# Attention weights of the last token tile transposed by VectorE and a round trip through DRAM, in a two-layer decoder trunk on one Trainium2 core

## The chip, the cores and the metric

The kernel runs on one core of a Trainium2 chip. The metric is the device time of one execution in microseconds (us), lower is better. Engines are named as in the profile: PE is TensorE (PEld its weight loads), DVE is VectorE, ACT is ScalarE, POOL is GpSimd, SP is SyncE, which here only issues DMAs.

## The reference

A trunk of two layers, each followed by a squared-ReLU MLP. Layer 0 mixes tokens by causal pooling, layer 1 by stick-breaking attention, with 16 heads of 64 and keys and values projected once from the stream behind layer 0. SEQ is 512, D_MODEL 1024, D_FF 4096, all in float32.

```python
def stick_breaking_attention(q, k, v):
    for i in range(S // Q_BLOCK):
        ...
        z = jnp.einsum('bhqd,bhkd->bhqk', q_blk, k_blk, ...) * inv_sqrt_d
        mask = s_idx < t_idx
        log1m = jnp.where(mask, -jax.nn.softplus(z), 0.0)
        excl = lax.cumsum(log1m, axis=3, reverse=True) - log1m
        a = jnp.where(mask, jnp.exp(jax.nn.log_sigmoid(z) + excl), 0.0)
        outs.append(jnp.einsum('bhqk,bhkd->bhqd', a, v_blk.astype(jnp.float32)))

def reference(x, ...):
    for layer in range(DEPTH):
        h = rms_norm(x, mix_pre_g[layer])
        m = ...                      # pooling (layer 0), or attention and w_o (layer 1)
        x = x + rms_norm(m, mix_post_g[layer])
        h = rms_norm(x, mlp_pre_g[layer])
        x = x + rms_norm(sq_relu_mlp(h, w_up[layer], w_down[layer]), mlp_post_g[layer])
        if layer == N_A - 1:
            kv = jnp.matmul(rms_norm(x, kv_norm_g), w_kv)...
    return x
```

## The kernel before

The 512 tokens are T = 4 tiles of 128. A float32 operand is split in two parts, hi (a cast, on ACT, L414) and lo (the rest, a subtraction on DVE, L415), and a product of two such operands is three products on PE (hi hi, hi lo, lo hi). The MLPs and the projections take most of the span.

The attention works on 8 pairs of heads. Its order is written out by hand in the table ATT_ORDER: each entry is a letter, a pair and sometimes a head of the pair (0 or 1), and a loop issues the entries one after the other under a manual schedule of all five engines. So the table alone sets the order on each engine. The letters that matter:

- S: scores of a pair (L1202), 24 products on PE into six PSUM banks, in three groups (token tile 3; tile 2; tiles 1 and 0); three rounds for each tile (hi hi, q hi with k lo, q lo with k hi), the two heads in turn
- G: sigmoids of the scores on ACT, `u` (L1216) and `w` (L1220) for both heads
- X: the running product along the keys, a scan on DVE over 1280 columns (L1225), into `e`. The 1280 columns are the causal part of a head's 512 x 512 weights, in segments: token tile 3 with 512 keys first, then tile 2 (384), tile 1 (256), tile 0 (128)
- M: `w = w * e` on DVE (L1316): a head's attention weights, tokens on partitions, keys along the columns
- T: the weights are transposed in blocks of 128 x 128 on PE (L1241), ten a head, through three PSUM banks, each copied by ACT (L1243) to a tile `at`: keys on partitions, tokens along the columns
- A: `mix_pair` (L1251), the product of a pair's weights with v: for each of the four key tiles s and each head one matmul over the tokens s*128 to 511, all in one PSUM bank. In float32 a matmul leaves two records in the trace. a: its split into `ohl` (ACT hi, DVE lo)
- J and Q: projections of k and q for a later pair (L842 to L844), 24 products each; j and q: their splits
- L, g, W, w: a weight of a later projection is loaded (SP, L223, into `raw`, `spare` or `late`), scaled by a gain (DVE, L230, 128 x 1024; only those for k and q), cast to hi (ACT, L249) and its lo taken (DVE, L258)
- Z, z: the output projection, 18 products a half and token tile for three pairs of heads

A pair's pieces are spread over two blocks of the table. S, G, X, M of pair p stand in one block with J, Q of pair p+1 and A of pair p-1; T of p closes the block; A of p comes at the end of the next. So on PE the steady order is A(p-1), T(p), S(p+1), J, Q, A(p), and so on. PSUM has eight banks of 128 x 512, given out in turn.

The functions that the change touches:

Of the kernel before, what the change touches and what calls it, by code (L numbers as in the profile page):

```python
# [10 lines left out]
F32 = mybir.dt.float32  # L11
# [4 lines left out]
P = 128  # L16
D = 1024
S = 512
T = S // P
KC = D // P  # L20
# [8 lines left out]
PAIRS = HEADS // 2  # L29
WINDOWS = (2, 4, 8, 16)  # L30
EPS = 1e-6
TS = [slice(t * P, (t + 1) * P) for t in range(T)]
NS = [slice(0, 512), slice(512, 1024)]
# [22 lines left out]
    (w[0], int(w[1:2] or 0), int(w[2:] or 0))  # L56
    for w in """V5 N2 v5 V0 N3 V3 F3 v0 J0 v3 F2 j0 Q0 L L q0 V1 v1 F1 L L V2 v2
    S0 G0 X00 M00 J1 W X01 w V4 M01 j1 T00 T01 W F4 v4 w Q1 q1 V6 v6
    S1 G1 g g X10 M10 X11 J2 L L M11 W j2 w Q2 q2 A0 a0 T10 T11 W
    S2 G2 g g w X20 M20 X21 J3 M21 W j3 w L L Q3 q3 A1 a1 T20 T21 W  # L60
    S3 G3 g g w X30 M30 X31 J4 M31 W j4 w L L Q4 q4 A2 a2 T30 T31 W
    S4 G4 g g w X40 M40 X41 J5 M41 W j5 w L Q5 q5 A3 a3 T40 T41 W
    S5 G5 w L L X50 M50 X51 J6 M51 W j6 w L Q6 q6 A4 a4 T50 T51 W
    S6 G6 w X60 M60 X61 J7 M61 W j7 w L L L Q7 q7 A5 a5 T60 T61 W
    S7 A6 G7 w L X70 Z002 M70 W X71 w Z102 M71 W T70 w R a6 W w L W Z034 Z134 w T71 L W w L Z055 Z155
    W w L A7 W w Z066 Z166 z206 a7 W w s""".split()
]

# [22 lines left out]
def trunk(ctx, tc, x, consts, gcol, grow, pw, wup, wdn, wq, wk, wv, wo, out):  # L91
    nc = tc.nc
# [5 lines left out]
    dram = pool("dram", space=bass.MemoryType.DRAM)  # L98
# [3 lines left out]
    def name(s):  # L102
        uid[0] += 1
        return f"{s}{uid[0]}"

    def ps():
        return psum.tile([P, 512], F32, tag="ps", name=name("ps"))
# [13 lines left out]
    turn = [0]  # L121
# [15 lines left out]
    behind, latest = {}, {}  # L137
# [19 lines left out]
    def gains(lo, n):  # L157


        def scaled(raw):  # L160
            for k in range(n):
                c = raw[:, k * D // n : (k + 1) * D // n]
                nc.scalar.mul(c, c, gc[:, lo + k : lo + k + 1])

        return scaled
# [44 lines left out]
    def late_next(what, fits=lambda x: True):  # L210
        while not fits(late[upto[what]]):
            upto[what] += 1
        upto[what] += 1
        return late[upto[what] - 1]
# [8 lines left out]
        nc.sync.dma_start(raw, x["src"])  # L223
        x["raw"] = raw

    def late_scale():
        x = late_next("g", lambda x: x["wide"] is not None)
        c = x["raw"].rearrange("p (k c) -> p k c", k=KC)
        g = gc[:, x["wide"] : x["wide"] + KC].unsqueeze(2).broadcast_to((P, KC, D // KC))
        nc.vector.tensor_tensor(out=c, in0=c, in1=g, op=ALU.mult)  # L230
# [134 lines left out]
    def fill(n=1):  # L365
        if gate[0]:
            behind.update(latest)
        for _ in range(n):
            if queue and sum(map(in_ring, made)) < ahead and (queue[0][0][0] != "dn" or dn_pool[0]):
                if not any(x["key"] == queue[0][0] for x in late) or queue[0][0] in kept:  # L370
                    make()
# [6 lines left out]
    for l in range(2):  # L378
        if l == 1:
            n = len(queue)  # L380
            for what, i, part in ATT_ORDER:
                if what == "V":
                    for h in range(2):
                        at = VALUES[i][2]
# [82 lines left out]
    class Update:  # L467
# [33 lines left out]
        def product(self, n):  # L501
            return self.beside if n and self.cuts is not NS else self.scaled
# [344 lines left out]
    with tc.tile_pool(name="mix0", bufs=1, reuse_waits="tile") as mp:  # L847
# [163 lines left out]
        def transposed(t, h):  # L1011
            pt = pts[t, h] = ps()
            for c in range(4):
                k = 4 * h + c
                nc.tensor.transpose(pt[:, TS[c]], xns[t][:, k * P : (k + 1) * P], ident)
# [47 lines left out]
    with tc.tile_pool(name="att", bufs=1, reuse_waits="tile") as ap:  # L1063
# [164 lines left out]
            )  # L1228
            return e

        def transposed(w):
            parts = {}
            for tiles in ((0,), (1, 3), (2,)):
                pt = ps()
                c = 0
                turned = ap.tile([P, S], F32, tag="at", bufs=6, name=name("at"))
                for s in tiles:
                    parts[s] = turned, c
                    for i in range(s, T):
                        at = SEG[i][0] + s * P  # L1240
                        nc.tensor.transpose(pt[:, c : c + P], w[:, at : at + P], ident)  # L1241
                        c += P
                latest["act"] = nc.scalar.copy(turned[:, :c], pt[:, :c])  # L1243
            return parts

        def mix_pair(p):
            po = pos[p] = ps()
            for s in range(T):
                for a in range(2):
                    turned, c = parts[p, a][s]  # L1250
                    nc.tensor.matmul(  # L1251
                        po[half[a], s * P :], v_all[:, s, 2 * p + a], turned[:, c : c + S - s * P],
                        start=s == 0, stop=s == T - 1, skip_group_check=True,
                    )

        def mixed_out(p):
            if p < PAIRS - 1:
# [24 lines left out]
        with tc.manual_schedule(engines={on.PE, on.Activation, on.DVE, on.Pool, on.SP}):  # L1282
            for what, i, a in ATT_ORDER:
                if what == "V":
                    value_product(i)
                elif what == "v":
                    value_out(i)
                elif what == "F":
                    form(i)
                elif what == "W":  # L1290
                    late_high()
                    if upto["W"] < 16:
                        fill()
                elif what in "Lgws":
                    {"L": late_load, "g": late_scale, "w": late_low, "s": late_store}[what]()
                elif what == "R":
                    gpost1, gpre1 = gain_row(R_MIX_POST1), gain_row(R_MLP_PRE1, spare_tile())
                elif what == "N":
                    need(i)
                elif what in "JQ":  # L1300
                    project(("k" if what == "J" else "q", i))
                    fill()
                elif what == "j":
                    keys(i)
                elif what == "q":
                    queries(i)
                elif what == "S":
                    pzs[i] = scores((qs[i], ks[i]))
                elif what == "G":
                    for a in range(2):  # L1310
                        ws[i, a] = sigmoids(pzs[i], a)
                elif what == "X":
                    es[i, a] = scanned(a)
                elif what == "M":
                    w = ws[i, a]
                    latest["dve"] = nc.vector.tensor_tensor(out=w, in0=w, in1=es.pop((i, a)), op=ALU.mult)  # L1316
                elif what == "T":
                    parts[i, a] = transposed(ws.pop((i, a)))
                elif what == "A":
                    mix_pair(i)  # L1320
                elif what == "a":
                    mixed_out(i)
                elif what in "Zz":
                    out_product(i, range(a // 10, a % 10 + 1), range(2) if what == "Z" else [0])
            assert upto["W"] == upto["w"] == len(late) and not going, upto
            ups = [Update(t, gpost1, None, gpre=gpre1) for t in range(T)]

            def evacuate(t, n):
                up, bank = ups[t], sums.pop((t, n))
                up.halves = (up.halves or []) + [ap.tile([P, 512], F32, tag="at", bufs=6, name=name("at"))]  # L1330
                up.just_square(n, bank)
                latest["dve"] = nc.vector.tensor_tensor(
                    out=up.halves[n], in0=bank, in1=gpost1[:, NS[n]], op=ALU.mult
                )

            for t in range(2):
                for n in range(2):
                    out_product(t, [PAIRS - 1], [n])
                    evacuate(t, n)
                ups[t].factor()  # L1340
            ups[0].sums_added()
            ups[0].rstd()
            ups[1].sums_added()
            ups[0].norm()
            ups[1].rstd()
            ups[1].norm()
            out_product(2, [PAIRS - 1], [0])
            evacuate(2, 0)
            out_product(2, range(PAIRS), [1])
            evacuate(2, 1)  # L1350
            ups[2].factor()
            out_product(3, range(PAIRS - 2), [0])
            ups[0].transpose()
            ups[2].sums_added()
            out_product(3, range(PAIRS - 2, PAIRS), [0])
            out_product(3, [0], [1])
            ups[1].transpose()
            evacuate(3, 0)
            ups[2].rstd()
            ups[2].norm()  # L1360
            out_product(3, range(1, PAIRS), [1])
            fill(4)
            evacuate(3, 1)
            ups[3].factor()
            ups[3].sums_added()
            ups[3].rstd()
            ups[3].norm()
            pending.update({t: ups[t] for t in (T - 2, T - 1)})
# [68 lines left out]
```

## Time and profile before

| | |
|---|---|
| median of 3 runs (lowest to highest) | 896.77 us (896.38 to 897.31) |
| profiled execution, its own time | 896.91 us |
| its span, first to last instruction | 895.1 us |
| busy: PE, DVE, ACT, POOL | 885.7, 689.4, 520.6, 85.1 us |
| the attention's pairs | one every 17.26 to 17.27 us, from A to A |
| transposes by PE in the attention (L1241) | 160, 19.3 us busy |

The profile's page gives busy times by engine, the chain of work that ended last, groups of instructions by line, and DMA issues with the time until they landed. A timeline row has the start, the duration, engine and line, the output and the inputs, the shape and the number of instructions, and in brackets how long the engine was idle before it and what released it. Times are counted from the span's start.

### The profile page before, as it was taken

The page shows a single profiled execution, that of the slowest core. Times are in us where ns is not written, and L with a number is a line of the kernel's source. Part 1 is how long each engine was busy: PE and PEld are TensorE (multiplying, and loading weights), DVE is VectorE, ACT ScalarE, POOL GpSimd, SP SyncE. Part 2 cuts the span into 40 slices and gives each one's busy share as a digit, 9 for nine tenths or more (in the row PEclk, how much of TensorE's full clock was granted, in tenths as well). Part 3 has the DMA queues.
Part 4 walks back from the last instruction along what each step waited for, and adds up shares of the span by engine and source line. Part 5 has one row for each costly group of instructions (what it writes and reads, how often), then busy time and mean ns, then how long its engine had stood idle before and what let it go on. Part 6 is the DMA issues. An engine that isn't in the chain of part 4 may idle for free.

```text
span 895.1 us, 11808 instructions
## 1 busy us (share of the span) xinstructions
PE 885.7 (99%) x4586; PEld 769.4 (86%) x4586; DVE 689.4 (77%) x705; ACT 520.6 (58%) x842; POOL 85.1 (10%) x83
## 2 busy tenths in 40 slices
PE   9999999999999999999999999999999999999996
PEld 7998888888888888888788888998888888888885
DVE  5966897998979967667887784765797776967866
ACT  6758557566888737345577564475445444544531
POOL 2100000000000005000000000120220400303103
PEclk9999999999999999999999999999999999999999
DMA  7453557369796820976122115333415043142102
GB/s 282 160 206 128 192 191 266 117 227 344 275 340 233 313 78 25 366 267 232 51 71 71 48 69 214 118 119 143 140 57 191 35 147 121 51 164 83 56 15 94
DMA packets 42349, 141.00 MB, mean 158 GB/s; under 512 B 4096, under 2 KB 4570, under 8 KB 42294
## 3 DMA queue, kind: packets, MB, share of 16 engines
q1 hardware_dynamic: 42146, 140.24, 43.7%
q8 instruction: 36, 0.59, 0.3%
q14 instruction: 19, 0.16, 0.1%
q10 hardware_dynamic: 148, 0.02, 0.0%
HBM read 116.12 MB, written 24.12 MB: 157 GB/s over the span
## 4 chain that ended last, share of the span: by engine, by line
PE 97%; DMA 1%; issue 1%; DVE 0%; ACT 0%; POOL 0%; POOLq 0%; DVEq 0%; SPq 0%; ACTq 0%
PE ps L726 28%; PE ps L842 16%; PE ps L843 15%; PE ps L844 15%; PE ps L1126 3%; PE ps L455 3%; PE ps L457 3%; PE ps L456 3%; PE ps L1251 2%; PE ps L1241 2%; PE ps L1202 2%; PE ps L981 2%; PE ps L957 1%; PE ps L544 1%; DMA w<-kept 1%
## 5 line engine op out<-in xcount | busy, mean ns | idle before, releaser
L726 PE MATMUL ps<-w,a 128*128 128x512 f32 x1176 | 265.3, 379 | 0.3
L842 PE MATMUL ps<-xnh,w 128*128 128x512 f32 (+1 forms) x704 | 253.5, 362 | 0.0
L844 PE MATMUL ps<-xnh,w 128*128 128x512 f32 (+1 forms) x704 | 253.1, 360 | 0.0
L843 PE MATMUL ps<-xnl,w 128*128 128x512 f32 (+1 forms) x704 | 253.1, 360 | 0.0
L726 PEld LDWEIGHTS ps<-w,a 128*128 128x128 f32 x1176 | 222.1, 189 | 32.5 <-ACT a L414 1.1
L844 PEld LDWEIGHTS ps<-xnh,w 128*128 128x128 f32 x704 | 133.4, 190 | 15.4
L843 PEld LDWEIGHTS ps<-xnl,w 128*128 128x128 f32 x704 | 133.4, 190 | 15.2
L842 PEld LDWEIGHTS ps<-xnh,w 128*128 128x128 f32 x704 | 132.8, 190 | 15.8
L152 ACT CAST w<-raw 128x1024 fp32r<-128x1024 f32 x56 | 58.5, 1045 | 83.9 <-PE ps L844 83.3
L738 DVE TENSOR_TENSOR y<-ps,y 128x512 f32<-128x512 f32 x124 | 83.2, 683 | 30.0 <-PE ps L726 29.9
L154 DVE TENSOR_TENSOR w<-raw,w 128x1024 fp32r<-128x1024 f32 x56 | 69.2, 1237 | 45.5 <-ACT w L152 45.5
L414 ACT CAST w<-e 128x1536 fp32r<-128x1536 f32 (+1 forms) x30 | 41.7, 1391 | 45.9 <-DVE e L699 34.4
L415 DVE TENSOR_TENSOR a<-r,a 128x768 fp32r<-128x768 f32 (+1 forms) x60 | 60.5, 1009 | 0.6 <-ACT a L414 0.6
L415 DVE TENSOR_TENSOR w<-e,w 128x1536 fp32r<-128x1536 f32 (+1 forms) x30 | 50.7, 1691 | 9.7 <-ACT w L414 9.5
L414 ACT CAST a<-r 128x768 fp32r<-128x768 f32 (+1 forms) x60 | 47.1, 785 | 17.9 <-POOL r L680 10.6
L1225 DVE TENSOR_TENSOR_SCAN e<-u,begin 128x1280 f32<-128x1280 f32 x16 | 45.2, 2825 | 13.3 <-ACT u L1216 12.5
L485 POOL TENSOR_TENSOR y<-y,grow 128x512 f32<-128x512 f32 x8 | 12.1, 1510 | 340.7 <-ACT xn L418 340.7
L414 ACT CAST w<-xn 128x1536 fp32r<-128x1536 f32 (+1 forms) x20 | 27.8, 1392 | 24.8 <-PE ps L726 24.8
L415 DVE TENSOR_TENSOR w<-w,w 128x1536 fp32r<-128x1536 f32 (+1 forms) x20 | 34.3, 1713 | 9.0 <-ACT w L414 8.9
L414 ACT CAST w<-w 128x1536 fp32r<-128x1536 f32 (+1 forms) x20 | 27.8, 1392 | 19.2 <-PE ps L726 19.2
L415 DVE TENSOR_TENSOR w<-xn,w 128x1536 fp32r<-128x1536 f32 (+1 forms) x20 | 33.0, 1648 | 7.1 <-ACT w L414 6.9
L761 ACT ACTIVATE r<-ps 128x512 f32<-128x512 f32 x56 | 33.0, 590 | 8.6 <-PE ps L844 8.6
(188 smaller groups left out, 1233.8 us busy)
## 6 DMA issues: line engine op xcount, KB each, us to landing
raw<-in_wup SPq DMA_DIRECT2D x63, 512.0 KB, 3.3
w<-kept SPq DMA_DIRECT2D x42, 512.0 KB, 5.6
w<-in_wdn SPq DMA_DIRECT2D x8, 1536.0 KB, 6.1
xn<-in_wdn SPq DMA_DIRECT2D x16, 768.0 KB, 4.5
kept<-wx SPq DMA_DIRECT2D x20, 512.0 KB, 3.5
kept<-apart SPq DMA_DIRECT2D x16, 512.0 KB, 3.8
apart<-in_wv SPq DMA_DIRECT2D x10, 512.0 KB, 5.1
raw<-in_wdn SPq DMA_DIRECT2D x8, 512.0 KB, 4.3
```

Of the source, the lines that this page charges most:

```text
L152: nc.scalar.copy(hi, raw)
L154: nc.vector.tensor_tensor(out=lo, in0=raw, in1=hi.bitcast(F32), op=ALU.subtract)
L414: latest["act"] = nc.scalar.copy(hi, src)
L415: latest["dve"] = nc.vector.tensor_tensor(out=lo, in0=src, in1=hi.bitcast(F32), op=ALU.subtract)
L455: nc.tensor.matmul(dst, ah, bh, start=start, stop=False)
L726: nc.tensor.matmul(bank, a[:, x, q, TS[t]], by_twos(w[:, z, q], NS[0]), start=start and q == 0 and k == 0, stop=q == self.n - 1 and k == 2 ...
L738: nc.vector.tensor_tensor(out=part, in0=bank, in1=part, op=ALU.add)
L761: nc.scalar.activation(split_up(r, 256), in_order(pu, 256), ACT.Relu)
L842: nc.tensor.matmul(pu[:, cols], wh[:, k, :], xh, start=k == 0, stop=False)
L843: nc.tensor.matmul(pu[:, cols], wh[:, k, :], xl, start=False, stop=False)
L844: nc.tensor.matmul(pu[:, cols], wl[:, k, :], xh, start=False, stop=k == KC - 1)
L1225: nc.vector.tensor_tensor_scan(out=e[:, ::-1], data0=us[a][:, 1:][:, ::-1], data1=begin[:, ::-1], initial=0.0, op0=ALU.mult, op1=ALU.max,)
```

## The change

In pairs 1 to 6 (TURNED) the last token tile (512 of a head's 1280 columns) is no longer transposed by PE. Directly behind each M, DVE transposes that segment in blocks of 32 x 32 (`turn_blocks`), both heads into one tile `turn`. A new step D (`quadrants`), behind T, puts the blocks in their place: one store of the tile to DRAM (`through`, 512 KB) and four loads of 32 partitions each (128 KB) into a tile `moved`, of which there is one. T then has six transposes a head, in two groups of three (128 x 384), so two copies by ACT instead of three. `mix_pair` takes the widths 384, 256 and 128 from `at`, and at its end eight products of 128 columns (four key tiles, two heads) from `moved`, read in four runs of 32 columns. Pairs 0 and 7 keep all ten transposes a head, in other groups; the third goes to the tile `moved`. `at` has 4 buffers of 384 columns in place of 6 of 512.

In blocks S1 to S4 one of the two g on DVE becomes c: the same scaling by ACT, as eight instructions of 128 x 128 between the casts of k and q. A6 moves from right behind S7 to behind Z002 and Z102 (36 products), just ahead of T70; its split a6 stays. `evacuate`, behind the attention, takes its tile from the room of v. POOL's order does not change.

```diff
-    S3 G3 g g w X30 M30 X31 J4 M31 W j4 w L L Q4 q4 A2 a2 T30 T31 W
+    S3 G3 g w X30 M30 X31 J4 M31 W j4 c w L L Q4 q4 A2 a2 T30 T31 D3 W
...
-    S7 A6 G7 w L X70 Z002 M70 W X71 w Z102 M71 W T70 w R a6 W w L W Z034 Z134 w T71 L W w L Z055 Z155
+    S7 G7 w L X70 Z002 M70 W X71 w Z102 M71 W A6 T70 w R a6 W w L W Z034 Z134 w T71 L W w L Z055 Z155
...
-    def late_scale():
+    def late_scale(on_scalar=False):
         x = late_next("g", lambda x: x["wide"] is not None)
+        if on_scalar:
+            gains(x["wide"], KC)(x["raw"])
+            return
...
-        def transposed(w):
+        Q, TURNED = P // 4, range(1, PAIRS - 1)
+        squares_of, moved = {}, {}
+        def turn_blocks(p, a):
+            if a == 0:
+                squares_of[p] = ap.tile([P, 4, 2, T, Q], F32, tag="turn", bufs=2, name=name("turn"))
+            out = squares_of[p][:, :, a].rearrange("p b j q -> p j b q")
+            src = ws[p, a][:, : T * P].rearrange("p (j b q) -> p j b q", b=4, q=Q)
+            latest["dve"] = nc.vector.transpose(out, src)
+        def quadrants(p):
+            src, dst = squares_of.pop(p), ap.tile([P, 4, 2, T, Q], F32, tag="moved", name=name("moved"))
+            through = dram.tile([4, Q, 4, 2 * T * Q], F32, tag=f"through{p}", name=name("through"))
+            nc.sync.dma_start(through.rearrange("b k c x -> (b k) c x"), src.rearrange("p c a j q -> p c (a j q)"))
+            for to in range(4):
+                nc.sync.dma_start(
+                    dst[Q * to : Q * to + Q].rearrange("p b a j q -> p b (a j q)"),
+                    through[:, :, to].rearrange("b k x -> k b x"),
+                )
+            return dst
+        def at_tiles(p, a):
+            if p in TURNED:
+                groups = (((0, T - 2),), ((1, T - 2), (2, T - 2)))
+            else:
+                groups = (((1, T - 1),), ((2, T - 1), (3, T - 1)), ((0, T - 1),))
+            for g, group in enumerate(groups):
+                if g < 2:
+                    yield group, ap.tile([P, 3 * P], F32, tag="at", bufs=4, name=name("at"))
+                else:
+                    if a == 0:
+                        moved[p] = ap.tile([P, 2, S], F32, tag="moved", name=name("at"))
+                    yield group, moved[p][:, a]
+        def transposed(p, a, w):
             parts = {}
-            for tiles in ((0,), (1, 3), (2,)):
+            for group, turned in at_tiles(p, a):
                 pt = ps()
                 c = 0
-                turned = ap.tile([P, S], F32, tag="at", bufs=6, name=name("at"))
-                for s in tiles:
-                    parts[s] = turned, c
-                    for i in range(s, T):
+                for s, last in group:
+                    parts[s] = turned, c, last
+                    for i in range(s, last + 1):
                         at = SEG[i][0] + s * P
                         nc.tensor.transpose(pt[:, c : c + P], w[:, at : at + P], ident)
                         c += P
@@ -1245,13 +1283,23 @@
         def mix_pair(p):
             po = pos[p] = ps()
+            def product(a, s, cols, moving, start, stop):
+                nc.tensor.matmul(
+                    po[half[a], cols], v_all[:, s, 2 * p + a], moving, start=start, stop=stop, skip_group_check=True,
+                )
+            whole = p not in TURNED
             for s in range(T):
                 for a in range(2):
-                    turned, c = parts[p, a][s]
-                    nc.tensor.matmul(
-                        po[half[a], s * P :], v_all[:, s, 2 * p + a], turned[:, c : c + S - s * P],
-                        start=s == 0, stop=s == T - 1, skip_group_check=True,
-                    )
+                    if s in parts[p, a]:
+                        turned, c, last = parts[p, a][s]
+                        cols = slice(s * P, (last + 1) * P)
+                        n = cols.stop - cols.start
+                        product(a, s, cols, turned[:, c : c + n], s == 0, whole and s == T - 1)
+            for s in () if whole else range(T):
+                for a in range(2):
+                    product(a, s, TS[T - 1], moved[p][:, :, a, s], False, s == T - 1)
...
+                elif what == "c":
+                    late_scale(True)
+                elif what == "D":
+                    moved[i] = quadrants(i)
...
+                    if i in TURNED:
+                        turn_blocks(i, a)
                 elif what == "T":
-                    parts[i, a] = transposed(ws.pop((i, a)))
+                    parts[i, a] = transposed(i, a, ws.pop((i, a)))
...
+            gained_rows = ap.tile([P, T, D], F32, tag="v", name="gained")
...
-                up.halves = (up.halves or []) + [ap.tile([P, 512], F32, tag="at", bufs=6, name=name("at"))]
+                up.halves = (up.halves or []) + [gained_rows[:, t, NS[n]]]
```

What the order shows, first on PE, from the mix of pair 2 over the transposes of pair 3 (`ps` are PSUM banks; before, four of the eight rows of the mix are left out):

```order
L1251 MATMUL ps_3806<-at_3660,v 64x256
L1251 MATMUL ps_3806<-at_3679,v 64x256
L1251 MATMUL ps_3806<-at_3653,v 64x128
L1251 MATMUL ps_3806<-at_3672,v 64x128
L1241 MATMUL ps_3818<-ident,w_3718 128x128 x4
L1241 MATMUL ps_3825<-ident,w_3718 128x128 x4
L1241 MATMUL ps_3832<-ident,w_3718 128x128 x2
L1241 MATMUL ps_3837<-ident,w_3726 128x128 x4
L1241 MATMUL ps_3844<-ident,w_3726 128x128 x4
L1241 MATMUL ps_3851<-ident,w_3726 128x128 x2
```

```order
L1288 MATMUL ps_3818<-at_3654,v 64x384
L1288 MATMUL ps_3818<-at_3666,v 64x384
L1288 MATMUL ps_3818<-at_3660,v 64x256
L1288 MATMUL ps_3818<-at_3672,v 64x256
L1288 MATMUL ps_3818<-at_3660,v 64x128
L1288 MATMUL ps_3818<-at_3672,v 64x128
L1288 MATMUL ps_3818<-moved_3678,v 64x128 x8
L1279 MATMUL ps_3837<-ident,w_3720 128x128 x3
L1279 MATMUL ps_3843<-ident,w_3720 128x128 x3
L1279 MATMUL ps_3849<-ident,w_3728 128x128 x3
L1279 MATMUL ps_3855<-ident,w_3728 128x128 x3
```

Six transposes a head stay, in groups of three; the mix ends with eight narrow products from `moved`, so it now also waits for DMAs.

On DVE, from the second head's M in one block to the first head's M in the next, before and after (`k`, `q`, `ohl` are lo parts; `spare`, `late` and `raw` loaded weights):

```order
L1225 SCALAR_TENSOR_TENSOR e_3740<-u_2967,begin 128x1280
L1316 TENSOR_TENSOR w_3726<-w_3726,e_3740 128x1280
L415 TENSOR_TENSOR k_3770<-ps_3742,k_3770 128x512
L258 TENSOR_TENSOR w_3768<-raw_3594,w_3768 128x1024
L415 TENSOR_TENSOR q_3803<-ps_3778,q_3803 128x512
L415 TENSOR_TENSOR ohl_3815<-ps_3806,ohl_3815 128x512
L230 TENSOR_TENSOR spare_3774<-spare_3774,gc 128x1024
L230 TENSOR_TENSOR late_3776<-late_3776,gc 128x1024
L258 TENSOR_TENSOR w_3856<-raw_3596,w_3856 128x1024
```

```order
L1244 STREAM_TRANSPOSE turn_3741<-w_3720 128x4x4x32
L1228 SCALAR_TENSOR_TENSOR e_3743<-u_2967,begin 128x1280
L1368 TENSOR_TENSOR w_3728<-w_3728,e_3743 128x1280
L1244 STREAM_TRANSPOSE turn_3741<-w_3728 128x4x4x32
L418 TENSOR_TENSOR k_3774<-ps_3745,k_3774 128x512
L261 TENSOR_TENSOR w_3772<-raw_3594,w_3772 128x1024
L418 TENSOR_TENSOR q_3815<-ps_3790,q_3815 128x512
L418 TENSOR_TENSOR ohl_3833<-ps_3818,ohl_3833 128x512
L233 TENSOR_TENSOR spare_3786<-spare_3786,gc 128x1024
L261 TENSOR_TENSOR w_3867<-raw_3596,w_3867 128x1024
L1228 SCALAR_TENSOR_TENSOR e_3920<-u_2966,begin 128x1280
```

A block transpose stands between M and the lo part of k, another behind the next M, and one of the two scalings by `gc` has left.

On SP, the late loads and the round trip (before, then after):

```order
L223 DMA raw_3594<-in_wk 128x1024
L223 DMA raw_3596<-in_wq 128x1024
L223 DMA spare_3774<-in_wk 128x1024
L223 DMA late_3776<-in_wq 128x1024
L223 DMA raw_3947<-in_wk 128x1024
L223 DMA raw_3949<-in_wq 128x1024
```

```order
L1249 DMA through_3679<-turn_3562 128x1024
L1251 DMA moved_3678<-through_3679 32x4x256 x4
L223 DMA spare_3786<-in_wk 128x1024
L223 DMA late_3788<-in_wq 128x1024
L1249 DMA through_3861<-turn_3741 128x1024
L1251 DMA moved_3860<-through_3861 32x4x256 x4
L223 DMA raw_3968<-in_wk 128x1024
L223 DMA raw_3970<-in_wq 128x1024
```

Each pair's store and four loads stand between the late loads, and what follows them in the queue waits behind their waits.

More of the change, by code (lines that the diff above doesn't have):

```diff
@@ L58 @@
     S0 G0 X00 M00 J1 W X01 w V4 M01 j1 T00 T01 W F4 v4 w Q1 q1 V6 v6
-    S1 G1 g g X10 M10 X11 J2 L L M11 W j2 w Q2 q2 A0 a0 T10 T11 W
-    S2 G2 g g w X20 M20 X21 J3 M21 W j3 w L L Q3 q3 A1 a1 T20 T21 W
-    S3 G3 g g w X30 M30 X31 J4 M31 W j4 w L L Q4 q4 A2 a2 T30 T31 W
-    S4 G4 g g w X40 M40 X41 J5 M41 W j5 w L Q5 q5 A3 a3 T40 T41 W
-    S5 G5 w L L X50 M50 X51 J6 M51 W j6 w L Q6 q6 A4 a4 T50 T51 W
-    S6 G6 w X60 M60 X61 J7 M61 W j7 w L L L Q7 q7 A5 a5 T60 T61 W
-    S7 A6 G7 w L X70 Z002 M70 W X71 w Z102 M71 W T70 w R a6 W w L W Z034 Z134 w T71 L W w L Z055 Z155
+    S1 G1 g X10 M10 X11 J2 L L M11 W j2 c w Q2 q2 A0 a0 T10 T11 D1 W
+    S2 G2 g w X20 M20 X21 J3 M21 W j3 c w L L Q3 q3 A1 a1 T20 T21 D2 W
+    S3 G3 g w X30 M30 X31 J4 M31 W j4 c w L L Q4 q4 A2 a2 T30 T31 D3 W
+    S4 G4 g w X40 M40 X41 J5 M41 W j5 c w L Q5 q5 A3 a3 T40 T41 D4 W
+    S5 G5 w L L X50 M50 X51 J6 M51 W j6 w L Q6 q6 A4 a4 T50 T51 D5 W
+    S6 G6 w X60 M60 X61 J7 M61 W j7 w L L L Q7 q7 A5 a5 T60 T61 D6 W
+    S7 G7 w L X70 Z002 M70 W X71 w Z102 M71 W A6 T70 w R a6 W w L W Z034 Z134 w T71 L W w L Z055 Z155
     W w L A7 W w Z066 Z166 z206 a7 W w s""".split()
```

## The prediction, made before the changed kernel ran

> **What bounds the kernel now.** I read the page first: busy time, then the chain of work that ended last.
>
> ```profile
> span 895.1 us, 11808 instructions
> PE 885.7 (99%) x4586; PEld 769.4 (86%) x4586; DVE 689.4 (77%) x705; ACT 520.6 (58%) x842; POOL 85.1 (10%) x83
> PE 97%; DMA 1%; issue 1%; DVE 0%; ACT 0%; POOL 0%; POOLq 0%; DVEq 0%; SPq 0%; ACTq 0%
> ```
>
> TensorE (PE) is busy for 99% of the span and 97% of the chain is PE's own work, so a microsecond less on PE is a microsecond off the time for as long as nothing else becomes late. Next I looked at the stage that the change touches: one whole pair, from one A (the product with v) to the next, by the table of busy times in a stretch and by PE's own timeline (start, duration, name, count; rows of J and Q are left out).
>
> ```profile
> 445.08:462.35 17.27, 17.27 (x110) 14.09 (x109) 15.11 (x12) 11.41 (x25) 0.00 (x0) 1.00 0.17 62
> ```
>
> The columns are length, then busy time of PE, PEld, DVE, ACT and POOL, PE's granted clock, DMA share and GB/s. PE has no gap at all in the 17.27 us; the clock is full; VectorE (DVE) is the second engine with 15.11 us, 87%, and the DMA engines are busy 17% of the time.
>
> ```profile
> 445.08 2.37 PE L1251 MATMUL ps<-at,v 128*64 128x512 f32 x16
> 447.39 2.40 PE L1241 MATMUL ps<-ident,w 128*128 128x128 f32 x20
> 449.72 2.14 PE L1202 MATMUL ps<-k,q 64*128 64x512 f32 x24
> 451.79 0.48 PE L842 MATMUL ps<-xnh,w 128*128 128x512 f32 x1
> ...
> 462.35 2.37 PE L1251 MATMUL ps<-at,v 128*64 128x512 f32 x16
> ```
>
> So a pair is A 2.31 us, T (20 transposes) 2.33, S (scores) 2.07, then 48 products of J and Q in 10.56, 0.22 each. Below, "A+x" is x us behind the start of a pair's A, here 445.08.
>
> **The transposes that go.** Per pair, T falls from 20 to 12 instructions.
>
> ```profile
> L1241 PE MATMUL ps<-ident,w 128*128 128x128 f32 x160 | 19.3, 275 | 0.0
> ```
>
> A transpose lasts 0.275 us, but they are pipelined: 20 of them take 2.40 from first start to last end, so 19 steps take 2.40 - 0.33 to 0.27, 0.109 to 0.112 each. At 0.109 the 8 that go are worth 0.87 us a pair, and 6 pairs 5.24 us. By the block's whole 2.33 / 20 = 0.1165 it would be 5.6. I take 0.109, since the change into and out of the block stays, and keep 5.6 for the low end.
>
> **The mix.** The last tile's columns leave the wide products (512, 384, 256, 128 columns become 384, 256, 128) and come back as four products of 128 columns a head. The number of columns stays. Are narrow products dearer? T's 20 instructions of 128 columns take 2.33 us, and A's 16 records, the same 20 units of 128 columns for each of two heads (run side by side), take 2.31. So the price goes by columns: +0.02 a pair, +0.1 in all. What no row shows is moving data in four runs of 32 values each, as the tile `moved` is read; its bound is a doubled rate (a rival).
>
> **The new work on DVE.** Two block transposes a pair (128 x 512 values each) come behind the M of each head, and one scaling g of 128 x 1024 leaves in each of four blocks. DVE in the pair shown, and the first row of the next:
>
> ```profile
> 445.52 0.69 DVE L415 TENSOR_TENSOR k<-ps,k 128x512 fp32r<-128x512 f32 x1
> 446.12 1.22 DVE L258 TENSOR_TENSOR w<-raw,w 128x1024 fp32r<-128x1024 f32 x1
> 447.25 0.68 DVE L415 TENSOR_TENSOR q<-ps,q 128x512 fp32r<-128x512 f32 x1
> 448.12 0.69 DVE L415 TENSOR_TENSOR ohl<-ps,ohl 128x512 fp32r<-128x512 f32 x1 [0.19 <-ACT ohl L414]
> 448.73 1.22 DVE L230 TENSOR_TENSOR spare<-spare,gc 128x1024 f32<-128x1024 f32 x1
> 449.86 1.22 DVE L230 TENSOR_TENSOR late<-late,gc 128x1024 f32<-128x1024 f32 x1
> 451.71 1.22 DVE L258 TENSOR_TENSOR w<-raw,w 128x1024 fp32r<-128x1024 f32 x1 [0.63 <-ACT w L249]
> 453.91 2.82 DVE L1225 TENSOR_TENSOR_SCAN e<-u,begin 128x1280 f32<-128x1280 f32 x1 [0.98 <-ACT u L1216]
> 456.87 1.49 DVE L1316 TENSOR_TENSOR w<-w,e 128x1280 f32<-128x1280 f32 x1
> 458.46 2.83 DVE L1225 TENSOR_TENSOR_SCAN e<-u,begin 128x1280 f32<-128x1280 f32 x1
> 461.42 1.49 DVE L1316 TENSOR_TENSOR w<-w,e 128x1280 f32<-128x1280 f32 x1
> 462.83 0.68 DVE L415 TENSOR_TENSOR k<-ps,k 128x512 fp32r<-128x512 f32 x1
> ```
>
> No row shows a block transpose. Call its time t. Below: the slope between the 128x1280 and 128x1024 products, (1.49 - 1.22) / 256 = 1.05 ns a column, without any fixed part, 0.54 us for 512. Above: the scan, the slowest row by column, 2.82 / 1280 = 2.2 ns, 1.13 us for 512. Nearest is a plain copy of 128x512:
>
> ```profile
> L735 DVE COPY y<-ps 128x512 f32<-128x512 f32 x4 | 2.6, 680 | 0.0
> ```
>
> I take t = 0.68: the same shape, one operand in and one out, as the new instruction. DVE's 15.11 becomes 15.11 + 2 x 0.68 - 1.22 = 15.25 of a period of 17.27 - 0.87 + 0.02 = 16.42: 93%, so it fits in sum. [...]
>
> Whether it fits in place is the sharper question: behind the second M stand k lo, w and q lo, and S waits for q lo. ACT sets when the first scan can start:
>
> ```profile
> 447.50 0.59 ACT L414 CAST ohl<-ps 128x512 fp32r<-128x512 f32 x1 [1.67 <-PE ps L1251]
> 448.14 2.61 ACT L1243 COPY at<-ps 128x512 f32<-128x512 f32 x6
> ...
> 451.52 0.66 ACT L1216 ACTIVATE u<-ps 128x511 f32<-128x511 f32 x1
> ...
> 453.23 0.65 ACT L1216 ACTIVATE u<-ps 128x255 f32<-128x255 f32 x2
> ...
> 458.23 0.58 ACT L414 CAST k<-ps 128x512 fp32r<-128x512 f32 x1
> 462.51 0.58 ACT L414 CAST q<-ps 128x512 fp32r<-128x512 f32 x1 [3.70 <-PE ps L844]
> ```
>
> Six copies of 2560 columns (2.61 us, 0.95 ns a column with the last one's tail off) become four of 1536, 0.97 us shorter; S starts 0.87 earlier. So u starts at A+5.47 instead of A+6.44, and the scan at A+7.86 instead of A+8.83. From the scan to the next k lo are 462.83 - 453.91 = 8.92 us, now 8.92 + 2t + 0.04. With the period of 16.4, k lo starts at the next A + 0.4 + 2t, and q lo ends 2.41 later (445.52 to 447.93). At t = 0.68 that is A+4.2. It is needed in the third round of S's products:
>
> ```profile
> 450.06 0.63 PE L1202 MATMUL ps<-k,q 64*128 64x512 f32 x4
> ```
>
> These four are rounds two and three, both heads side by side; the last began about 0.39 before the end, at 450.30, 0.57 into S. The new S starts at A+3.77, so q lo must be there at A+4.34. Before, it ended 2.4 us ahead of that point; after, 0.15 us. The bound on t is about 0.75. A late S gives DVE that much more time in the next pair, so I put 0.1 us in all on small stalls. Behind q lo, ohl lo (0.6) ends near A+4.8; the second PSUM bank of S's last group waits for it, near A+5.1 to 5.2. Then g (1.13) and w (1.22) end near A+7.2, ahead of the scan at A+7.86; with both g left in, they would have ended at A+8.3, behind it. That is the cover which moving one g to ScalarE buys.
>
> **The scaling on ACT (c).** Eight instructions of 128x128 stand between k hi and q hi, in the 3.70 us for which ACT waits ahead of q hi (row above).
>
> ```profile
> L163 ACT ACTIVATE apart<-apart,gc 128x128 f32<-128x128 f32 x56 | 17.1, 388 | 0.0
> ```
>
> 8 x 17.1 / 56 = 2.4 us: hidden, 1.3 us to spare; cost nothing. If that cover were gone, q hi would be late, and S with it.
>
> **The way through DRAM.** The store waits for the second block transpose, at about A+1.9; SP issues the loads only when the store has landed. The nearest issues (KB each, us to landing):
>
> ```profile
> kept<-apart SPq DMA_DIRECT2D x16, 512.0 KB, 3.8
> late<-in_wq SPq DMA_DIRECT2D x2, 512.0 KB, 8.1
> out<-x SPq DMA_DIRECT2D x2, 128.0 KB, 2.0
> ```
>
> Store landed by A+5.7, four issues at about a third of a us, landed by A+9.5. A reads `moved` last, behind 12 of its 20 units: 16.4 + 1.4 = A+17.8. So 8 us are to spare and it costs nothing. The late weight loads queued behind on SP start up to 5 us later; the scale or cast that reads them comes a pair later, so they are covered too. Tightest is pair 6, whose store is queued behind three late loads:
>
> ```profile
> 514.14 2.37 PE L1251 MATMUL ps<-at,v 128*64 128x512 f32 x16
> ...
> 520.85 2.38 PE L1251 MATMUL ps<-at,v 128*64 128x512 f32 x16
> ```
>
> In its old place A6 stands 6.7 us behind A5 (5.8 now), sooner than 9.5. Moved behind 36 products of 0.22, it stands at A5 + 13.7 and reads `moved` at 15.1; store from about 4, landed about 11.5. Moving A6 changes no amount of work.
>
> **The sum**, against the profiled execution (896.91 us, of which 1.8 lie outside the span): 895.1 - 5.24 + 0.1 + 0.1 = 890.1, plus 1.8 is 891.9. The median of the runs shown is 0.14 lower, 896.77; so 891.7.
>
> **The rivals.**
> 1. *DVE becomes late.* With t at the upper bound of 1.13, q lo ends at A+5.1, 0.8 us behind S's need; the late S leaves the next pair that much more time, so it is lost about every second pair, three times 0.8. In the four blocks with g DVE would have 15.11 + 2.26 - 1.22 = 16.15 of 16.4, with nothing left for its waits of some 0.4, so 0.1 to 0.2 more each. Together about 3: 894.5. For it: 0.15 us of slack is little. Against: the scan is slow by what it computes, and a transpose computes nothing. [...]
> 2. *Slower: `moved` comes late.* If each leg through DRAM took the slowest row's 8.1 us, the data would be there at 1.9 + 8.1 + 1.5 + 8.1 = A+19.6 against 17.8: PE waits 1.8 us in each of six pairs, 10.8 against a gain of 5.2: 902. It decides from legs of 7.2 us. Against: loads of 8.1 were queued beside other loads, and the DMA share here is 17%.
> 3. *No change: the strided reading of `moved` runs at half rate.* 8 rounds of 0.11 to 0.116 more a pair, 5.3 to 5.6 in all, eat the gain: 897. Nothing in the trace speaks for it but the lack of a row.
>
> **How the numbers follow.** My case 0.72, at 891.7, by itself 890.8 (transposes at 0.1165, and the runs' own spread of 0.4) to 892.6 (stalls of 0.15 a pair). Rival 1 0.13, rival 3 and larger mishaps that just eat the gain 0.07, rival 2 0.08. The range goes from 890.8 to 895.2, which takes in rival 1. About 0.2%, 1.8 us, is what a measurement of this kernel tells from no change: faster 0.84 (my case and nearly all of rival 1), same 0.08, slower 0.08.
>
> **What would show it.** T of a middle pair with 12 instructions in about 1.46 us; period 16.4; PE without gaps ahead of S; the block transpose at 0.68; scan at A+7.9; loads of `moved` landed about 8 us ahead of A's first use; eight ScalarE scalings ahead of q hi with over a us left. I would be wrong if S shows idle time released by DVE's q lo, if A shows idle time released by a DMA, or if A takes longer than 2.4 us.

## The result and the profile after

The changed kernel takes 891.9 us (median of 6 runs, 891.54 to 892.35); the kernel before took 897.25 us (median of 6 runs, 896.38 to 898.04). The ratio is 0.9941, with a 95% interval of 0.9929 to 0.9954. The profiled execution took 891.9 us, its span is 890.1 us, against 895.1 before. One execution in the first experiment below, its first profile, ran at a mean granted clock of 0.752 (1155 us) and is not counted.

The page after, its head and the chain:

```profile
span 890.1 us, 11934 instructions
PE 880.3 (99%) x4610; PEld 767.5 (86%) x4610; DVE 690.8 (78%) x713; ACT 523.9 (59%) x862; POOL 84.2 (9%) x83
PE 93%; DMA 3%; DVE 1%; ACT 1%; issue 1%; POOL 0%; POOLq 0%; DVEq 0%; SPq 0%; ACTq 0%
```

PE lost 5.4 us of busy time and the span 5.0; PE is still busy for 99% of it. The chain was 97% PE before; now it leaves PE between 526 and 558 us, around and behind the last pair, for late weight loads and what reads them (DMA 3%). PE has no gap there either, so nothing is lost, but the chain leaves these loads no time to spare, and the experiment that turns all pairs fails in that stretch. One pair of the changed kernel, from A to A, by the busy times in a stretch and by PE's timeline:

```profile
460.49:476.89 16.40, 16.40 (x113) 13.80 (x112) 15.10 (x13) 12.70 (x31) 0.00 (x0) 1.00 0.28 96
```

```profile
460.49 1.51 PE L1288 MATMUL ps<-at,v 128*64 128x384 f32 x12
461.83 1.04 PE L1288 MATMUL ps<-moved,v 128*64 128x128 f32 x16
462.81 1.53 PE L1279 MATMUL ps<-ident,w 128*128 128x128 f32 x12
464.27 2.14 PE L1205 MATMUL ps<-k,q 64*128 64x512 f32 x24
```

The pair takes 16.40 us instead of 17.27, with no gap on PE. T takes 464.27 - 462.81 = 1.46 instead of 2.33; A takes 2.32 instead of 2.31, the eight narrow products included. DVE around the same A, with the scan that follows:

```profile
461.40 0.71 DVE L1244 STREAM_TRANSPOSE turn<-w 128x512 f32<-128x512 f32 x1
462.04 0.65 DVE L418 TENSOR_TENSOR k<-ps,k 128x512 fp32r<-128x512 f32 x1
462.61 1.21 DVE L261 TENSOR_TENSOR w<-spare,w 128x1024 fp32r<-128x1024 f32 x1
463.74 0.68 DVE L418 TENSOR_TENSOR q<-ps,q 128x512 fp32r<-128x512 f32 x1
...
468.25 2.82 DVE L1228 TENSOR_TENSOR_SCAN e<-u,begin 128x1280 f32<-128x1280 f32 x1 [0.96 <-ACT u L1219]
```

The block transpose lasts 0.71 us (0.64 to the start of the next). q lo ends at 464.42, A+3.93, and S wants it 0.57 into its block, at 464.84: 0.42 us to spare. The scan starts at A+7.76, still behind ACT. ACT's scaling c, and the cast of q behind it:

```profile
473.26 2.44 ACT L163 ACTIVATE raw<-raw,gc 128x128 f32<-128x128 f32 x8
477.06 0.59 ACT L417 CAST q<-ps 128x512 fp32r<-128x512 f32 x1 [1.36 <-PE ps L847]
```

ACT is done 1.36 us before q hi's operand comes from PE.

SP's queue in this pair:

```profile
462.14 0.33 SPq L1249 DMA_DIRECT2D through<-turn  x1
464.77 1.76 SPq L1251 DMA_DIRECT2D moved<-through  x4
466.62 0.38 SPq L223 DMA_DIRECT2D spare<-in_wo  x1
```

The store was issued at A+1.65 and its loads from A+4.28 on, 2.6 us later. A load lands 2.5 to 3.3 us after its issue, so `moved` is there by 466.5 + 3.3, about A+9.3. The next A wants it at 476.89 + 1.34, A+17.7. For pair 6 the queue is tightest:

```profile
513.48 0.98 SPq L1249 DMA_DIRECT2D through<-turn  x1
519.12 1.76 SPq L1251 DMA_DIRECT2D moved<-through  x4
```

This store, right behind a late load, took 5.6 us until the loads could go. In the kernel with A6 in its old place, below, the loads went out 0.29 us later and let PE go at 523.76, so here they had landed by about 523.5. A6 reads them at 524.88, some 1.4 us later.

### The profile page after: what moved, and what is told of

Read it like the earlier page. It is cut to its first block, busy times and chain, and to the rows that moved or that the text cites. A ratio compares the mean times of both kernels' runs of the same rounds, so it can differ in the third digit from the quotient of the medians.

```text
span 890.1 us, 11934 instructions
## 1 busy us (share of the span) xinstructions
PE 880.3 (99%) x4610; PEld 767.5 (86%) x4610; DVE 690.8 (78%) x713; ACT 523.9 (59%) x862; POOL 84.2 (9%) x83
## 4 chain that ended last, share of the span: by engine, by line
PE 93%; DMA 3%; DVE 1%; ACT 1%; issue 1%; POOL 0%; POOLq 0%; DVEq 0%; SPq 0%; ACTq 0%
PE ps L729 28%; PE ps L845 16%; PE ps L846 16%; PE ps L847 16%; PE ps L1129 3%; PE ps L458 2%; PE ps L460 2%; PE ps L459 2%; PE ps L1205 2%; PE ps L1288 2%; PE ps L984 2%; PE ps L1279 1%; DMA raw<-in_wup 1%; PE ps L960 1%; PE ps L547 1%
```

## The experiments

**Is the gain PE's own, with nothing lost to the work that replaces it?** One kernel without that work, profiled twice:

```diff
         def turn_blocks(p, a):
-            ...
+            return
         def quadrants(p):
-            ...
+            dst = ap.tile([P, 4, 2, T, Q], F32, tag="moved", name=name("moved"))
+            nc.gpsimd.memset(dst.rearrange("p b a j q -> p (b a j q)"), 0.0)
+            return dst
```

> The changed kernel without the work that replaces the transposes: no block transposes on DVE, no way through DRAM; moved is only set to zero by GpSimd (the last token tile's attention is left out). PE's instructions stay those of the changed kernel. Theory (PE's own instructions set the time, the added DVE and DMA work is hidden): the same as the changed kernel, 891.9 us, span 890.1 to within 0.3, pair period 16.40. Rival (some of the 5.24 to 5.6 us was given back to small stalls behind the added work): span shorter by 0.4 or more, 889.7 or less.

> The same kernel as no_side, for a profile at full clock: span 890.0 to within 0.3 of the changed kernel's 890.1, pair period 16.40 (theory), or 889.7 and less (rival).

Three runs took 891.72 to 891.92 us; the second profile took 892.2 us with a span of 890.4. Its A's, one pair apart:

```profile
444.48 1.52 PE L1278 MATMUL ps<-at,v 128*64 128x384 f32 x12
...
460.88 1.51 PE L1278 MATMUL ps<-at,v 128*64 128x384 f32 x12
```

The same 16.40. Without the block transposes and the round trip the kernel is no faster, so all of that work is hidden and nothing was given back to it.

**How much room has the way through DRAM?**

```diff
+            if p < 5:
+                again = dram.tile([P, D], F32, tag=f"again{p}", name=name("again"))
+                flat = dst.rearrange("p b a j q -> p (b a j q)")
+                nc.sync.dma_start(again, flat)
+                nc.sync.dma_start(flat, again)
             return dst
```

> In pairs 1 to 4 the tile moved goes once more through DRAM behind its four loads (one store of 512 KB, one load of 512 KB into the same tile), so A's data land later and the late loads queued on SP start later. Theory (the way through DRAM has about 9 us to spare: landed near A+9, wanted at the next A + 1.35, which is A+17.75; one more store and load take about 6.5): no change, 891.9 us within 0.5. Rival (SP's delay of the late weight loads by 6.5 us starves a scaling or cast, or moved lands too late): PE waits in some of the four pairs, 1 us or more in all, 893 or above.

891.74 us (891.62 to 892.08), ratio to before 0.9944 (0.9929 to 0.9959), span 889.9; no wait of PE on `moved`. One more store and load of 512 KB in four pairs cost nothing, although the late loads behind them went out 5.6 to 5.8 us later (472.40 instead of 466.62 in the pair above). The rival, that SP's delay of the weight loads is felt, falls for these pairs.

**What when `moved` does come late?** A6 in its old place, and 18 products later than that:

```diff
-    S7 G7 w L X70 Z002 M70 W X71 w Z102 M71 W A6 T70 ...
+    S7 A6 G7 w L X70 Z002 M70 W X71 w Z102 M71 W T70 ...      (a6_old)
+    S7 G7 w L X70 Z002 A6 M70 W X71 w Z102 M71 W T70 ...      (a6_mid)
```

> The changed kernel with A6 in its old place right behind S7. Theory (A waits for the loads of moved when they are late, and nothing of such a wait on PE is made up): pair 6's loads land about 523.2 on the changed kernel's clock, A6's products from moved would be due at 516.9, so PE waits 6.2 to 6.5 us: 898.1 to 898.4, slower than the kernel before the change. Rival (the stage behind S7 has its own waits that take this up, or the loads come sooner when they are waited for): less than 3 us lost, under 895.

> A6 between Z002 and Z102, 18 products later than its old place. Its products from moved are due at about 520.8 on the changed kernel's clock, the loads land at about 523.5, so PE waits about 2.7 us. In the kernel with A6 in its old place PE waited 6.4 us and then ran at a granted clock of 0.50 for 5.6 us, which cost 2.8 more. Theory 1 (a wait of some 2.7 us is long enough to bring the clock down too): 2.7 + about 2.8, 897.4 us. Theory 2 (the clock falls only behind longer waits): 2.7 alone, 894.6 us.

A6 in its old place gives 901.01 us (900.3 to 901.22), slower than before: ratio 1.0044 (1.0027 to 1.006). The wait is the size expected, the loss is not. PE's timeline and its waits by line:

```profile
PE ps L1288 <- DMA moved<-through: 6.4, 1, 6.4
```

```profile
515.84 1.52 PE L1288 MATMUL ps<-at,v 128*64 128x384 f32 x12
523.76 1.97 PE L1288 MATMUL ps<-moved,v 128*64 128x128 f32 x16 [6.41 <-DMA moved<-through]
```

The 16 records from `moved` took 1.97 us, not 1.04. The stretches show why (PE's granted clock stands behind POOL's busy time):

```profile
500.00:515.00 15.00, 15.00 (x99) 12.52 (x99) 13.22 (x11) 8.83 (x22) 0.00 (x0) 1.00 0.34 119
523.76:525.66 1.90, 1.90 (x16) 1.57 (x16) 1.90 (x2) 0.00 (x0) 0.00 (x0) 0.50 0.17 67
525.66:529.10 3.44, 3.44 (x10) 2.81 (x9) 3.13 (x3) 0.00 (x0) 0.00 (x0) 0.50 0.00 0
529.30:545.00 15.70, 15.70 (x84) 13.94 (x83) 3.05 (x3) 6.02 (x10) 0.00 (x0) 1.00 0.42 135
```

Behind the wait PE had half its clock (0.50) for 5.3 to 5.6 us, which costs 2.7 to 2.8 us more: 6.4 + 2.8 = 9.2, the span's 899.3 - 890.1. So nothing of the wait was made up, and the rival falls. With A6 in the middle:

```profile
PE ps L1288 <- DMA moved<-through: 2.6, 1, 2.6
```

```profile
523.55:525.25 1.70, 1.70 (x17) 1.37 (x17) 1.70 (x2) 0.00 (x0) 0.00 (x0) 0.58 0.23 92
525.25:526.90 1.65, 1.65 (x5) 1.37 (x5) 1.65 (x2) 0.00 (x0) 0.00 (x0) 0.50 0.00 0
527.00:535.00 8.00, 8.00 (x43) 7.03 (x43) 3.40 (x5) 3.73 (x6) 0.00 (x0) 0.98 0.33 131
```

Its profile (895.86 us, span 894.1) shows the lower clock (0.58, then 0.50) behind a wait of 2.6 us, for 3.3 us: 2.6 + 1.5 = 4.1 against 4.0 in the span. But its five runs fall in two groups, 893.13 to 893.46 (three) and 895.86 and 896.43, median 893.46. Theory 1 holds for the profiled run, with a shorter spell of low clock than expected. The three faster runs left no trace, but they lost only 1.2 to 1.6 us against the changed kernel, less than a wait of 2.6 alone, so if nothing else was won, PE waited less in them. Their mean granted clock was 0.997, against 0.995 and 0.996 in the two others and 0.998 to 0.999 in the changed kernel; whether it fell at all behind their wait stays open.

**Is DVE's slack as small as the sum had it?**

```diff
-            latest["dve"] = nc.vector.transpose(out, src)
+            for _ in range(2):
+                latest["dve"] = nc.vector.transpose(out, src)
```

> Each block transpose on DVE is done twice (the same values again), 0.63 us more in sequence each, 1.26 a pair. Theory (DVE's chain from scan to q lo has 0.4 us of slack, not more): PE waits ahead of S for q lo, about 0.45 us in each pair from the second on, since a late S also moves the next pair's start: 2 to 2.7 us in six pairs, 893.9 to 894.6, and the waits of PE name DVE q (L418) ahead of S. Rival A (DVE is busy only 78% of the time, so it has room): 891.9. Rival B (DVE is the bound by its sum alone, 16.6 against a period of 16.4 in four blocks): 892.7.

895.26 us (894.91 to 895.75), 3.4 more than the changed kernel; ratio to before 0.9982 (0.9972 to 0.9991). PE's waits, the head of one pair in its timeline, and the busy times of the pair ahead of it and of a later one:

```profile
PE ps L1205 <- DVE q L418: 2.0, 6, 0.4
```

```profile
462.23 1.52 PE L1289 MATMUL ps<-at,v 128*64 128x384 f32 x12
463.58 1.04 PE L1289 MATMUL ps<-moved,v 128*64 128x128 f32 x16
464.55 1.53 PE L1280 MATMUL ps<-ident,w 128*128 128x128 f32 x12
466.01 0.74 PE L1205 MATMUL ps<-k,q 64*128 64x512 f32 x4
467.12 1.68 PE L1205 MATMUL ps<-k,q 64*128 64x512 f32 x20 [0.37 <-DVE q L418]
```

```profile
445.24:462.23 16.99, 16.66 (x113) 13.71 (x112) 16.48 (x15) 12.70 (x31) 0.00 (x0) 1.00 0.34 124
479.29:496.27 16.98, 16.66 (x113) 13.71 (x112) 15.41 (x14) 10.34 (x23) 0.00 (x0) 1.00 0.42 155
```

S does its first two rounds and waits for q lo ahead of the third, in all six blocks behind a turned pair. The third round starts 1.11 us into S instead of 0.57, and the pair takes 16.99 us, 0.59 more: 6 x 0.59 = 3.5. It is a bit above what was expected because two transposes into one tile take 1.39 us in sequence where one takes 0.64, 1.5 more a pair and not 1.26, and because PE's busy time in the pair is 0.26 longer beside the gap of 0.33, with the same instructions. Only about half of what lies beyond the slack is lost in each pair, (1.5 - 0.42) / 2 = 0.54 by this estimate: a late S also gives DVE more time in the next pair.

Rival A (room by the busy share) falls. So does rival B (the sum alone), which the first of the two pairs shown could not tell, since DVE hardly rests in it. The second pair has no scaling in its block: DVE is busy for 15.41 of 16.98 us and waits 0.97 for ACT's `u`, and still the pair is as long. The chain to q lo decides.

**Does one scaling have to leave DVE?**

```diff
-    S3 G3 g w X30 M30 X31 J4 M31 W j4 c w L L ...
+    S3 G3 g g w X30 M30 X31 J4 M31 W j4 w L L ...
```

> The changed kernel with both scalings g of blocks S1 to S4 on DVE again, none on ScalarE. Rival (the prediction's reading: this cover is what keeps the first scan on time): scan 0.4 us late in each of four blocks, 1.6 to 1.8 us lost, about 893.6. Theory, from the profile after: DVE ends the last lo part about 0.9 us ahead of the scan, and a scaling takes 1.13 us in sequence, so the scan is only 0.1 to 0.3 us late, and q lo has 0.4 us to spare ahead of S, which takes most of it up: 891.9 to 892.4.

891.81 us (891.75 to 891.92), ratio to before 0.9944 (0.9929 to 0.9958), span 889.9: no loss. Its A is at 460.65; DVE behind q lo:

```profile
463.94 0.68 DVE L418 TENSOR_TENSOR q<-ps,q 128x512 fp32r<-128x512 f32 x1
464.55 0.68 DVE L418 TENSOR_TENSOR ohl<-ps,ohl 128x512 fp32r<-128x512 f32 x1
465.14 2.35 DVE L233 TENSOR_TENSOR raw<-raw,gc 128x1024 f32<-128x1024 f32 x2
467.41 1.22 DVE L261 TENSOR_TENSOR w<-late,w 128x1024 fp32r<-128x1024 f32 x1
468.54 2.82 DVE L1228 TENSOR_TENSOR_SCAN e<-u,begin 128x1280 f32<-128x1280 f32 x1
```

DVE has no gap left ahead of the scan, which starts at A+7.89 instead of A+7.76. That 0.13 is taken up: q lo ends at 464.62, S (at 464.43) wants it at 465.00.

**Can the other two pairs be turned as well?** Pair 0 at first right behind each M, then both pairs, then pair 0 alone with its transposes behind the splits of v and q:

```diff
-        Q, TURNED = P // 4, range(1, PAIRS - 1)
+        Q, TURNED = P // 4, range(PAIRS - 1)                      (pair0, pair0_late; all_pairs: range(PAIRS))
...
+    ... M01 j1 T00 T01 D0 W F4 v4 ...                             (pair0, all_pairs)
+    ... V6 v6 D0                                                  (pair0_late: both transposes in D0)
+    ... Z102 M71 W A6 D7 T70 ...                                  (all_pairs)
```

> Pair 0's last token tile is also turned by DVE and goes through DRAM (a D0 behind T01). Theory (8 transposes fewer are worth 8 x 0.109 = 0.87 us wherever the chain is PE's): 891.0 us, span 889.2. Rival (the block of pair 0 has DVE filled with the splits of v, so a block transpose there delays S1 or the first k): no gain, 891.9 or more.

> All eight pairs are turned: pair 0 as in the kernel beside it, pair 7 with D7 between A6 and T70. Theory: 16 transposes fewer than the changed kernel, 1.75 us, so 890.15 us, span 888.4. Rival (pair 7's loads wait for the one tile moved, which A6 frees at about 526, and land behind A7's need at about 537; or DVE's two transposes in S7 delay T70): PE waits ahead of A7 or T70 and the gain is 0.9 or less, 891.0 or more.

> Pair 0 turned as well, but its two block transposes stand behind the splits of v and of q (D0 behind v6), where DVE sat idle 5.2 us ahead of the next scan, not right behind each M. Theory (pair 0's turn cost time only because it stood ahead of the M and the splits that T01 and the last product of v wait for): the 1.26 us of waits on PE go, the 0.87 us of transposes stay won: 891.0 us, span 889.2, faster than the changed kernel. Rival (any further work in pair 0's block, the loads through DRAM on SP among it, costs as much as it brings): 891.9 or more.

Pair 0: 893.07 us (892.93 to 894.09), 1.2 more than the changed kernel. PE's waits:

```profile
PE ps L1279 <- DVE w L1368: 0.6, 1, 0.6
PE ps L1129 <- DVE v L1145: 0.6, 1, 0.6
```

The rival was right: T01 waits for the second M, a product of v for a split of v, both behind the new transposes on DVE; these 1.26 us, less the 0.87 won, make up 0.4 of the 1.2, and if each wait cost some 0.2 more than it shows, as those above did, 0.8. Moved behind those splits, both waits are gone and the time is 891.84 us (891.22 to 892.16, span 890.2), the changed kernel's, where 891.0 was expected. PE reached the next S 0.37 us earlier than in the changed kernel (414.70 against 415.07), less than half of 0.87; at PE's last product of the span (882.35 against 882.60) 0.25 us were left, too little to measure. That T01 now comes too soon for the second M, which ends at 403.27, when T00's six transposes from 402.49 on are done, may explain part of it; this was read from the trace and not tried.

All pairs: 899.09 us (898.49 to 900.18), slower than before, ratio 1.0025 (1.0016 to 1.0035). The waits that pair 0 brings are there, but the large one is elsewhere. PE's waits, ACT's timeline and SP's:

```profile
PE ps L458 <- ACT ohl L417: 3.6, 1, 3.6
```

```profile
542.23 1.04 ACT L252 CAST w<-raw 128x1024 fp32r<-128x1024 f32 x1 [8.00 <-DMA raw<-in_wup]
...
547.92 1.04 ACT L252 CAST h<-raw 128x1024 fp32r<-128x1024 f32 x1 [3.41 <-DMA raw<-in_wo]
548.87 0.58 ACT L417 CAST ohl<-ps 128x512 fp32r<-128x512 f32 x1
```

```profile
529.77 0.34 SPq L1249 DMA_DIRECT2D through<-turn  x1
532.83 1.74 SPq L1251 DMA_DIRECT2D moved<-through  x4
...
535.62 1.41 SPq L223 DMA_DIRECT2D raw<-in_wup  x2
```

```profile
551.50:553.50 2.00, 2.00 (x6) 1.61 (x5) 1.07 (x1) 0.00 (x0) 0.00 (x0) 0.50 0.92 363
```

A7 itself did not wait. D7 held SP's queue while its store landed, so the loads of the up projection went out at 535.62 (530.56 in the changed kernel). ACT's casts of these weights waited for them, and the next load, of the output projection, went out at 544.56 instead of 538.85; the split of A7's result stood behind the cast of that load on ACT, and PE behind that split. Behind this wait of 3.6 us, too, PE had half its clock (0.50 in the last row, PE's stretch behind it), from about 551 to 554; with 0.86 in the 2.0 us ahead of that row and 0.83 in the 2.5 us behind it this costs some 1.7 us. Up to A7 this kernel is 0.2 us behind the changed one (536.18 against 535.96); of the 6.4 us more from there on, the wait and the clock make up 5.3, and the rest is not traced. So SP's delay of the late loads, harmless in pairs 1 to 6, is what forbids the same step in pair 7.

## Why the prediction was right

- *The transposes that go.* 0.87 us a pair by the spacing of 0.109; T went from 2.33 to 1.46, 0.87. Right. The whole-block price of 0.1165 did not apply.
- *The mix.* +0.02 a pair was forecast, and A took 2.32 instead of 2.31. Reading `moved` in four runs of 32 cost nothing; rival 3 falls by this row. Its doubled rate was the author's assumption, which no row shows.
- *The block transpose.* t = 0.68 was taken from the copy, 0.71 measured, 0.64 in sequence. The two bounds of 0.54 and 1.13 held it. 512 values a partition took 0.64 us in sequence, 1.25 ns each, against the 1.05 ns a column of DVE's products. DMAs off the critical path put the 32x32 blocks in place here, and the kernel before, which turns these segments on PE, is 5 us slower.
- *DVE's place.* The scan at A+7.86 was forecast, A+7.76 measured; q lo's end A+4.2, measured A+3.93; slack 0.15, measured 0.42. So no stalls, and the 0.1 us put on them was not needed. The chain that rival 1 rests on is real: doubling the transposes made PE wait for q lo, six times, and about half of the lateness was felt in each pair, as rival 1 had it.
- *The scaling on ACT.* That it costs nothing was right (eight in 2.44 us, 1.36 us to spare ahead of q hi). That moving it buys the cover was wrong: with both g on DVE the time stays. The step had q lo's end at A+4.2 (A+3.97 measured in that kernel) and let the scan wait for the whole duration of w, 1.22, where it follows 1.13 behind w's start. So w ended at A+7.98 and not A+8.3, the scan was 0.13 us late and not 0.4, and q lo's slack took that up.
- *The way through DRAM.* 8 us of room were forecast, 8.4 measured, and one more trip was free. That A6 had to move was right: in its old place it waits 6.4 us. The room of pair 6 was mis-sized: its loads were to land at A5+11.5, 3.6 us ahead of their use, and landed at about A5+13.8, 1.4 us ahead of it, because the store took 5.6 us and not 3.8. Rival 2 counted its waits of 1.8 us alone. Behind waits of 6.4, 3.6 and once 2.6 us the clock was down too (0.50), so its price may have been too low; no run has a wait of 1.8.
- *The sum.* The span was to fall to 890.1 and fell to 890.1; 891.7 was forecast, 891.9 measured; by the medians of runs side by side the gain is 5.35 us, where 5.07 were forecast. That the terms came out right is shown above; that the sum agrees to 0.1 us is in part luck. From A of pair 0 to A of pair 7 the changed kernel took 108.27 us (427.69 to 535.96) instead of 113.26 (427.82 to 541.08), 4.99 less, where 5.04 were forecast, and outside of it it is 0.13 shorter ahead and 0.12 longer behind. The 0.1 for stalls was not needed, while the block of S7, where moving A6 was put at nothing, took 22.47 us from S to A7 instead of 22.30. What these 0.17 us are was not traced.

## What to carry to other kernels

Where PE has no gap, price an instruction by its spacing in the stream and not by its duration (0.109 us and not 0.275 for a transpose here), and then look for the one operand of the next block that the new work stands ahead of: the room is the time between that operand's end and its use (0.42 us here), not the idle share of the engine (22%). A round trip through DRAM was free here (16.40 us a pair with it and without) where its data were wanted a whole period later and nothing urgent was queued behind it on the same DMA queue; where a cast and a split stand behind a delayed load, as behind the last pair, it cost more than it brought (899.09 us with the last pair turned as well as pair 0, 893.07 with pair 0 alone). And a wait of several microseconds on PE cost more than its length: 9.2 us for 6.4, 5.3 for 3.6 and, in one profile, 4.1 for 2.6.

## What the runs showed of the hardware

PE's granted clock fell to half behind three waits, of 6.4, 3.6 and 2.6 us. Behind 6.4 us of idle time it was 0.50 for about 5.5 us, behind 3.6 us for about 3 us, and in one profile behind 2.6 us it was 0.50 to 0.58 for about 3.3 us; in the kernel with doubled transposes, with waits of 0.3 to 0.4 us, it stayed at 1.00. How long a wait has to be for this was not measured.
